# Operand sums by accumulating transfers in a hybrid attention and gMLP block on one Trainium2 core

## The chip, the cores and the metric

The kernel runs on one core of a Trainium2 chip. The core has a matrix engine (PE, with its weight loads shown as PEld), a vector engine (DVE), a scalar engine (ACT), a general engine (POOL) and a queue engine (SP), each of which works through its own instructions in order and waits on semaphores for the others. Transfers are started by an instruction of an engine's queue (here SP's and POOL's above all) and carried out by 16 DMA engines. The metric is the device time of one execution in microseconds, lower is better.

## What is computed

One layer of a streaming encoder on 1024 tokens of width 1024, in float32. Cut to what matters here (`sgo` is the gMLP branch, `a` the attention branch):

```python
h = rmsnorm(x, norm_g[l])
proj = h @ w_in[l]
q, k, v, za, u, vs, zs, gm = jnp.split(proj, IN_SPLITS, axis=-1)
a = window_sink_attention(q, k, v, att_sinks[l])
a = (a * jax.nn.silu(za)) @ w_att_out[l]
sgo = chunked_spatial_gating(gelu(u), gelu(vs), sg_w[l], sg_b[l], sg_ln_g[l], sg_ln_b[l])
sgo = (sgo * jax.nn.silu(zs)) @ w_sg_out[l]
ga, gs = jnp.split(jax.nn.sigmoid(gm + b_merge[l]), N_BRANCHES, axis=-1)
y = ga * a + gs * sgo
x = x + y @ w_o[l]
return rmsnorm(x, final_g)
```

## The kernel before

**Products.** Every large product is done by one level of Strassen's method in Winograd's form: seven products of quarters in place of eight. The moving operand of a stage (the activations, feature by token) is cut into four quarters q11, q12, q21, q22 of 512 x 512, and seven *forms* are made of them: b11 = q11, t1 = q11 - q12, t2 = -(q22 + q11 - q12), b21 = q21, t3 = q22 - q12, b22 = q22, t4 = q22 + q11 - q12 - q21. To keep float32 accuracy each form is split into a rounded high part and a low part that holds the rest (`split`, line 152: ACT writes the high part, DVE subtracts it from the source to write the low part), and a product is three matmuls per 128 rows: high by high, high by low, low by high. `product` (line 338) issues the twelve matmuls of one of the seven products.

**Pairs.** `gemm_pair` (line 355) makes two output blocks of 128 features by 1024 tokens: seven `product`s in the order b11, t1, t2, b21, t3, b22, t4, with the evictions between them (ACT: the copies to x11, x22 and x12; DVE: the sums at lines 376, 381 and 385), a call of `finish` for each of the four output tiles, and a call of `hook` after each product (seven in a pair). `split_next` (line 212), called four times in a pair, splits the weights of the pair to come into `wh` and `wl` (three buffers each). The x tiles come from a ring of five; each is free again when its store has landed. After the t2 product the x12 copy has to read the accumulator before the t3 product adds to it.

**Stages.** The work around the change has three stages of four pairs each (m = 0, 2, 4, 6). The *za stage* multiplies the input projection `hb` and applies SiLU; `finish_silu` (line 1598) multiplies each tile by the attention output, loaded as a gate tile from `at_dr`, and stores it to `a_dr` through POOL's queue. In its gaps `parts_of_s` (line 1540) makes the gMLP branch's operand: it loads the quarters of `z_dr` into `s_q`, applies SiLU and multiplies by the rows of `s1_dr`; the rows of quarter (1, 0), which is q21, come last, one by one in `multiply_row`. A table, read by (m, hook number), says when each step is written. The *s stage* multiplies the forms of `s_q` (`sb_`) and gates with the sigmoid of `gs_dr`; meanwhile the quarters of `a_dr` are loaded into `a_q`. The *a stage* multiplies the forms of `a_q` (`ab`) and gates with `ga_dr`; `y_dr` collects both.

**The boundaries.** `forms_of` (line 1506) makes the forms of a new operand, for s between the za and s stages and for a between the s and a stages. The four sums are made in place by DVE (`combine`, line 187, two instructions of 128x1024 each, seen in the profile as bq from bq and bq): q12 := q11 - q12, then q12 := q22 + q12, q11 := q12 - q11, q21 := q12 - q21. Each is followed by the splits of its form (`fill_b`, line 182). Every form has one buffer, high and low, so a fill may only be written when the last pair of the stage before has used that form. All seven are written ahead of the first pair of the new stage.

**What sets the order.** The program is written in sequence; a planner at compile time then draws up each engine's order from readiness and priority, and the position in the program is the priority. `after(second, first)` asks that `second` come behind `first` in that order. At run time each engine keeps its order and waits where something isn't ready. `want_gate` (line 1537) loads a gate tile into one of the tags g0 to g3 in turn (g0 and g1 alone in the za stage, while g2 and g3 hold the rows of `s1_dr`), and the load waits until the last reader of that tag is done.

Of the kernel before, what the change touches and what calls it, by code (L numbers as in the profile page):

```python
# [27 lines left out]
ALU = mybir.AluOpType  # L28
# [5 lines left out]
KC = D // P  # L34
# [18 lines left out]
def hybrid_tile(  # L53
# [97 lines left out]

    def split(hi, lo, src, minus=False):
        if minus:
            nc.scalar.mul(hi, src, -1.0)
            nc.vector.scalar_tensor_tensor(
                lo, src, -1.0, hi.bitcast(F32), op0=ALU.mult, op1=ALU.subtract
            )
        else:
            hi_of.append(nc.scalar.copy(hi, src))  # L159
            return nc.vector.tensor_sub(lo, src, hi.bitcast(F32))  # L160
# [20 lines left out]

    def fill_b(b, name, src, minus=None):
        hi, lo = b[name]
        for c in range(0, 4, 2):
            split(hi[:, c : c + 2, :], lo[:, c : c + 2, :], src[:, c : c + 2, :], name == "t2" if minus is None else minus)

    def combine(op, dst, a, c):
        for i in range(0, 4, 2):
            op(dst[:, i : i + 2, :], a[:, i : i + 2, :], c[:, i : i + 2, :])  # L189

# [13 lines left out]
    def begin_job():  # L206
        n = len(begun)
        if n < written[0]:
            begun.append(n)
            units.extend(jobs[n]())  # L210

    def split_next():

        if not units:
            begin_job()
        if not units:
            return
        halves, keys = units.pop(0)
        if keys[0][1] == 2:
            make_sums(term_of_x11[0] if done[0] <= 4 else None)  # L220
        hi = mtile([P, D], F32R, "wh", 3)
        lo = mtile([P, D], F32R, "wl", 3)
        if isinstance(halves, list):
            for c, half in enumerate(halves):
                split(hi[:, half_of(c)], lo[:, half_of(c)], half)
        else:
            wide = halves.shape[1]
            first = split(hi[:, 0:wide], lo[:, 0:wide], halves)
            if keys[0] == (done[0] - 1, 6) and done[0] > LAST_OF_Q + 2:
                make_sums(first)  # L230
        for c, key in enumerate(keys):
            ready[key] = hi[:, half_of(c)], lo[:, half_of(c)]
        if len(units) == 1:
            begin_job()
# [22 lines left out]
    def make_sums(first=None):  # L257

        while sums_to_make:
            sums_to_make.pop(0)(first)  # L260
# [203 lines left out]
    def get(src, m, half, bufs, tag="g"):  # L464
        g = mtile([P, HALF], F32, tag, bufs, pool)
        copy_to(g[:], place(src, m, half))
        return g
# [1035 lines left out]
            fill_b(b, name, o_loaded[name], False)  # L1503
            yield b

    def forms_of(qs):
        q11, q12, q21, q22 = (qs[k] for k in QUARTERS)
        b = {}

        def fill(name, q):  # L1510
            b.update(new_b((name,)))
            fill_b(b, name, q)

        combine(nc.vector.tensor_sub, q12, q11, q12)
        yield
        fill("b11", q11)
        fill("t1", q12)
        combine(nc.vector.tensor_add, q12, q22, q12)
        fill("t2", q12)
        fill("b21", q21)  # L1520
        combine(nc.vector.tensor_sub, q11, q12, q11)
        fill("t3", q11)
        fill("b22", q22)
        combine(nc.vector.tensor_sub, q21, q12, q21)
        fill("t4", q21)
        yield b

    ORDER = ((0, 0), (1, 1), (0, 1), (1, 0))
    gates = []

    turn = [0]

    def gtag(among=4):
        turn[0] += 1
        return f"g{turn[0] % among}"

    def want_gate(src, m, half, among=4):
        gates.append(get(src, m, half, 1, gtag(among)))

    def parts_of_s():  # L1540

        factors, of_rows = [], {}

        def rows(src, j, half):
            return src[:].rearrange("(c p) t -> p c t", p=P)[:, 4 * j : 4 * j + 4, half_of(half)]

        def load(j, half):
            s_q[j, half] = q = bq()  # L1550
            copy_to(q[:], rows(z_dr, j, half))

        def load_factors(j, half):
            factors.append(bq(0))
            copy_to(factors[-1][:], rows(s1_dr, j, half))

        def silu(j, half):
            for c in range(0, 4, 2):
                v = s_q[j, half][:, c : c + 2, :]
                after(nc.scalar.activation(v, v, AF.Silu), pace[0])  # L1560

        def multiply(j, half, c):
            v = s_q[j, half][:, c : c + 2, :]
            after(nc.vector.tensor_mul(v, v, factors[-1][:, c : c + 2, :]), term[0])

        def load_row(c, half):
            of_rows[c, half] = get(s1_dr, 4 + c, half, 1, f"g{2 + c % 2}")

        def multiply_row(c, half):
            v = s_q[1, half][:, c, :]  # L1570
            after(nc.vector.tensor_mul(v, v, of_rows[c, half][:]), term[0])

        return {
            (0, 1): [(load, 0, 0), (load_factors, 0, 0)],
            (0, 2): [(load, 1, 1)],
            (0, 3): [(load, 0, 1)],
            (0, 4): [(load_row, 0, 1), (load_row, 1, 1)],
            (0, 5): [(silu, 0, 0)],
            (0, 6): [(multiply, 0, 0, 0)],
            (0, 7): [(multiply, 0, 0, 2), (load_factors, 0, 1), (silu, 1, 1)],  # L1580
            (2, 1): [(multiply_row, 0, 1), (multiply_row, 1, 1), (load_row, 2, 1), (load_row, 3, 1)],
            (2, 3): [(silu, 0, 1)],
            (2, 6): [(multiply, 0, 1, 0), (multiply_row, 2, 1)],
            (2, 7): [(multiply, 0, 1, 2), (multiply_row, 3, 1), (load, 1, 0), (load_row, 0, 0), (load_row, 1, 0)],
            (4, 6): [(silu, 1, 0)],
            (4, 7): [(multiply_row, 0, 0), (multiply_row, 1, 0), (load_row, 2, 0), (load_row, 3, 0)],
            (6, 6): [(multiply_row, 2, 0), (multiply_row, 3, 0)],
        }


# [6 lines left out]

    def finish_silu(q, m, half):

        after(nc.vector.tensor_mul(q[:], q[:], gates.pop(0)[:]), term[0])  # L1600
        put(a_dr, m, half, q[:], nc.gpsimd)
        if of_att:
            want_gate(at_dr, *of_att.pop(0), 2)

    def part_of_s(m):
        of_za[0] += 1
# [5 lines left out]
    for m in range(0, KC, 2):  # L1612
        if m == 0:
            for _ in range(2):
                want_gate(at_dr, *of_att.pop(0), 2)
        if m == 6:
            s_forms = forms_of(s_q)
            next(s_forms)

        def finish(i, half, q, src, sign):  # L1620
            pace[0] = nc.scalar.activation(q[:], src, AF.Silu, scale=sign)
            silus.append((q, m + i, half))

        gemm_pair(hb, finish, lambda: part_of_s(m), "tp")
# [4 lines left out]

    def gate_of(src, m, i, half, col):  # L1630

        g = gates.pop(0)
        c = col + m + i
        gate = nc.scalar.activation(g[:], g[:], AF.Sigmoid, bias=bm_sb[:, c : c + 1])

        after(gate, pace[0])
        return g
# [8 lines left out]
    for m in range(0, KC, 2):  # L1646
        if m == 2:
            a_q = {}
            ahead_of_time += loads_of_quarters(a_q, a_dr)
        if m == 6:  # L1650
            a_forms = forms_of(a_q)
            next(a_forms)

        def finish(i, half, q, src, sign):
            gated(q, src, sign, gate_of(gs_dr, m, i, half, KC))
            put(y_dr, m + i, half, q[:], nc.gpsimd)
            want_gate(*((gs_dr, m + 2 + i, half) if m < 6 else (ga_dr, i, half)))

        gemm_pair(sb_, finish, part_of_loads, "tp")
    ab = next(a_forms)  # L1660


# [62 lines left out]
    for m in range(0, KC, 2):  # L1725
        if m == 6:
            written[0] += 1
            had = [mtile([P, D], F32, "s", 2) for _ in range(2)]
            for i in range(2):
                copy_to(had[i][:], y_dr[(m + i) * P : (m + i + 1) * P, :])  # L1730

        def finish(i, half, q, src, sign):
            gated(q, src, sign, gate_of(ga_dr, m, i, half, 0))
            if m < 6:
                add_to(place(y_dr, m + i, half), q[:])
                want_gate(ga_dr, m + 2 + i, half)
            else:
                nc.vector.tensor_add(q[:], q[:], had[i][:, half_of(half)])
                if half == 1:
                    last_rows[i] = q  # L1740
                copy_to(place(y_dr, m + i, half), q[:])

        if m == 2:
            ahead_of_time += [lambda name=name: load_o(name, paced) for name in list(O_SOURCES)[:4]]
        gemm_pair(ab, finish, lambda: part_of_loads(3), "tp")
    written[0] = len(jobs)

    fill = o_forms()
# [211 lines left out]
```

## Time and profile before

| | us |
|---|---|
| median of 3 runs | 908.18 |
| the runs | 908.16, 908.18, 910.48 |
| the profiled execution, its own time | 911.38 |
| the profiled execution, first to last instruction | 909.6 |

A row of the order of time gives the start, the duration, the engine, the line of the kernel, the operation, output from inputs, the shape, and in brackets how long the engine had been idle and what ended that. L346 is the matmul of `product`, L159 and L160 are the high and low parts in `split` (L155 the low part of a negated form), L189 the sums of `combine`, L204 loads through SP's queue, L462 stores, L201 and L559 accumulating transfers. A row of the waits gives the waiting engine and what it waited for, then total, count and longest. A transfer's "to landing" is counted from its issue. The granted clock in the profile is the share of PE's full speed.

### The profile page before, as it was taken

Reading aid. Unit: us, or ns where it says so; the run is one execution under the profiler, and the core shown is the slowest. Engines: PE = TensorE matmul, PEld = TensorE weight load, DVE = VectorE, ACT = ScalarE, POOL = GpSimd, SP = SyncE. Lnnn points to the kernel's source line nnn. Section 1 sums busy time; section 2 is a strip of 40 time slices with the busy share of each in tenths; the row PEclk is TensorE's granted clock in tenths of the full one; section 3 lists DMA queues with packets and bytes.
Section 4 is the critical chain, followed back from the end, with each engine's and each line's share of the span. In section 5 each row is a group of like instructions: output and inputs, shape, how many; then the busy total and the mean of one; then the engine's idle time right before and its main releaser. Section 6 shows DMA issues by size and latency. Waiting matters only on the chain.

```text
span 909.6 us, 13196 instructions
## 1 busy us (share of the span) xinstructions
PE 895.0 (98%) x4290; PEld 745.0 (82%) x4290; DVE 698.1 (77%) x1264; ACT 530.0 (58%) x1061; POOL 143.3 (16%) x205
## 2 busy tenths in 40 slices
PE   9999999999999999999999999999998999999996
PEld 6888888888888888888888888888877887888885
DVE  6869966666686778888778788647797589479996
ACT  7875533334545566767668667554674385367443
POOL 2322222203030001111111011201001111110012
PEclk9999999999999999999999999999999999999999
DMA  9997888958778667788686789899869665998632
GB/s 327 212 259 209 264 207 172 173 156 270 251 250 286 206 181 203 215 185 210 158 243 214 239 223 251 217 345 344 291 194 363 224 188 167 313 298 267 208 117 115
DMA packets 131598, 209.57 MB, mean 230 GB/s; under 512 B 12649, under 2 KB 61033, under 8 KB 131530
## 3 DMA queue, kind: packets, MB, share of 16 engines
q1 hardware_dynamic: 110072, 149.74, 50.1%
q0 software_dynamic: 21312, 58.73, 28.2%
q8 instruction: 34, 0.56, 0.3%
q14 instruction: 34, 0.28, 0.1%
q10 hardware_dynamic: 146, 0.27, 0.1%
HBM read 147.74 MB, written 86.11 MB: 257 GB/s over the span
## 4 chain that ended last, share of the span: by engine, by line
PE 87%; DVE 8%; DMA 2%; issue 2%; ACT 1%; SPq 0%; DVEq 0%; ACTq 0%
PE ps_mm L346 36%; PE ps_o L346 27%; PE ps_sc L1290 3%; PE ps_tp L346 3%; PE ps_mm L703 2%; PE ps_o L703 2%; PE ps_tp L703 2%; PE ps_o L1375 2%; PE ps_tp L1334 2%; PE ps_sc L346 2%; PE ps_tp L965 2%; DVE wl L160 1%; PE ps_sc L703 1%; DVE bq L189 1%; DMA wr<-in_w_dram 1%
## 5 line engine op out<-in xcount | busy, mean ns | idle before, releaser
L159 ACT CAST wh<-s 128x1024 fp32r<-128x1024 f32 (+1 forms) x79 | 79.3, 1006 | 95.6 <-PE ps_mm L346 51.3
L160 DVE TENSOR_TENSOR wl<-wr,wh 128x512 fp32r<-128x512 f32 (+1 forms) x77 | 72.0, 936 | 53.6 <-ACT wh L159 53.0
L160 DVE TENSOR_TENSOR wl<-s,wh 128x1024 fp32r<-128x1024 f32 (+1 forms) x79 | 92.6, 1172 | 12.2 <-ACT wh L159 11.9
L159 ACT CAST wh<-wr 128x512 fp32r<-128x512 f32 (+1 forms) x77 | 63.1, 821 | 59.3 <-PE ps_mm L346 30.7
L346 PE MATMUL ps_o<-T_t1h,wh 128*128 128x512 f32 x148 | 58.9, 398 | 0.8 <-ACT wh L159 0.7
L346 PE MATMUL ps_o<-T_b22h,wh 128*128 128x512 f32 x148 | 58.3, 394 | 0.0
L346 PE MATMUL ps_mm<-T_b11h,wl 128*128 128x512 f32 x140 | 55.4, 396 | 2.9 <-DVE wl L160 2.9
L346 PE MATMUL ps_o<-T_t1h,wl 128*128 128x512 f32 x148 | 57.9, 391 | 0.3 <-DVE wl L160 0.3
L346 PE MATMUL ps_o<-T_b22l,wh 128*128 128x512 f32 x148 | 57.9, 391 | 0.0
L346 PE MATMUL ps_o<-T_b22h,wl 128*128 128x512 f32 x148 | 57.8, 390 | 0.0
L346 PE MATMUL ps_o<-T_t1l,wh 128*128 128x512 f32 x148 | 57.7, 390 | 0.0
L1303 ACT ACTIVATE pr<-ps_sc,sm 128x192 f32<-128x192 f32 (+2 forms) x128 | 50.7, 409 | 9.0 <-DVE sm L1299 6.6
L346 PE MATMUL ps_mm<-T_b11h,wh 128*128 128x512 f32 x140 | 55.4, 395 | 0.0
L346 PE MATMUL ps_mm<-T_t4h,wh 128*128 128x512 f32 x140 | 55.2, 395 | 0.0
L346 PE MATMUL ps_mm<-T_t3l,wh 128*128 128x512 f32 x140 | 54.6, 390 | 0.6 <-DVE T_t3l L160 0.6
L346 PE MATMUL ps_mm<-T_b11l,wh 128*128 128x512 f32 x140 | 55.2, 394 | 0.0
L346 PE MATMUL ps_mm<-T_t3h,wh 128*128 128x512 f32 x140 | 55.0, 393 | 0.0
L346 PE MATMUL ps_mm<-T_t4h,wl 128*128 128x512 f32 x140 | 54.8, 391 | 0.0
L346 PE MATMUL ps_mm<-T_t3h,wl 128*128 128x512 f32 x140 | 54.7, 390 | 0.0
L346 PE MATMUL ps_mm<-T_t2h,wl 128*128 128x512 f32 x140 | 54.6, 390 | 0.0
L346 PE MATMUL ps_mm<-T_t2h,wh 128*128 128x512 f32 x140 | 54.6, 390 | 0.0
L346 PE MATMUL ps_mm<-T_t2l,wh 128*128 128x512 f32 x140 | 54.6, 390 | 0.0
(394 smaller groups left out, 2402.8 us busy)
## 6 DMA issues: line engine op xcount, KB each, us to landing
wr<-in_w_dram SPq DMA_DIRECT2D x86, 256.0 KB
sums<-in_w_dram POOLq DMA_DIRECT2D x20, 512.0 KB, 6.8
s<-sums SPq DMA_DIRECT2D x20, 512.0 KB
q_hl<-qhl SPq DMA_DIRECT2D x16, 512.0 KB
q<-q_hl SPq DMA_DIRECT2D x64, 128.0 KB
y_dr<-x POOLq DMA_DIRECT2D x28, 256.0 KB, 6.7
g<-in_w_dram POOLq DMA_DIRECT2D x12, 512.0 KB, 6.4
wr<-in_w_dram SPq DMA_DIRECT2D x11, 512.0 KB
```

The lines of the kernel that those rows point to most:

```text
L159: hi_of.append(nc.scalar.copy(hi, src))
L160: return nc.vector.tensor_sub(lo, src, hi.bitcast(F32))
L189: op(dst[:, i : i + 2, :], a[:, i : i + 2, :], c[:, i : i + 2, :])
L346: nc.tensor.matmul(acc, lt, rt, start=fresh and k == 0 and n == 0, stop=k == 3 and n == 2, skip_group_check=True,)
L703: mm = nc.tensor.matmul(acc[:], lt, rt, start=fresh and k == 0 and n == 0, stop=k == 3 and n == terms[-1], skip_group_check=True,)
L965: nc.tensor.matmul(pm[:, t * P : (t + 1) * P], xh[:, half * 4 + t, g * P : (g + 1) * P], bias[-1][1][:, g % 4, :], start=True, stop=True,)
L1290: nc.tensor.matmul(sc[:, i, k0:], q_of[:, c, i * P : (i + 1) * P], kt[:, f, k0:], start=f == 0, stop=f == 1,)
L1303: nc.scalar.activation(held_in[c, i], sc[:, i, lo:hi], AF.Exp, bias=nmax[:, c, i : i + 1], scale=-1.0, accum_out=sums[:, c, i : i + 1],)
L1334: nc.tensor.transpose(dst, pr[:, i, block * P : block * P + width], ident[:])
L1375: nc.tensor.matmul(po[:, cs], lt, rt, start=n == 0, stop=n == len(terms) - 1)
```

## The change

Two of the four sums move from DVE to accumulating transfers on POOL's queue: q12 += q22, and minus21 += q12. For the second the quarter q21 is kept negated: the last multiplication of its rows carries a factor of -1 (`times`), in `multiply_row` for s and in `finish_silu` for a, and b21's form negates it back. T2's high parts are put behind the last but one weight cast (`of_units`), the t3 sum behind t2's low parts. The t4 form is no longer made ahead of the new stage but at the third hook of its first pair (`last_form`), its high parts behind the x12 copy. The last two rows of q21 for s, with their place in the table moved from hook 6 to hook 2 of the last pair, are put behind t1's low parts; when they are done their tags g2 and g3 go to the last two `at_dr` gates (`more_gates`), and gate tags are kept in a list of free ones.

```diff
     def split(hi, lo, src, minus=False):
         if minus:
-            nc.scalar.mul(hi, src, -1.0)
-            nc.vector.scalar_tensor_tensor(
+            hi_of.append(nc.scalar.mul(hi, src, -1.0))
+            return nc.vector.scalar_tensor_tensor(
                 lo, src, -1.0, hi.bitcast(F32), op0=ALU.mult, op1=ALU.subtract
             )
...
+        of_units.append(hi_of[-1])
...
-    def forms_of(qs):
-        q11, q12, q21, q22 = (qs[k] for k in QUARTERS)
+    def forms_of(qs, behind_t1=()):
+        q11, q12, minus21, q22 = (qs[k] for k in QUARTERS)
         b = {}
 
-        def fill(name, q):
+        def fill(name, q, minus=None):
             b.update(new_b((name,)))
-            fill_b(b, name, q)
+            return fill_b(b, name, q, minus)
+
+        def add_aside(dst, src):
+            for i in range(0, 4, 2):
+                add_to(dst[:, i : i + 2, :], src[:, i : i + 2, :])
 
         combine(nc.vector.tensor_sub, q12, q11, q12)
         yield
         fill("b11", q11)
-        fill("t1", q12)
-        combine(nc.vector.tensor_add, q12, q22, q12)
-        fill("t2", q12)
-        fill("b21", q21)
-        combine(nc.vector.tensor_sub, q11, q12, q11)
+        low = fill("t1", q12)[-1]
+        for move in behind_t1:
+            after(move, low)
+        add_aside(q12, q22)
+        fill("b21", minus21, True)
+        low = fill("t2", q12)[-1]
+        for hi in hi_of[-2:]:
+            after(hi, of_units[-2])
+        add_aside(minus21, q12)
+        for sub in combine(nc.vector.tensor_sub, q11, q12, q11):
+            after(sub, low)
         fill("t3", q11)
         fill("b22", q22)
-        combine(nc.vector.tensor_sub, q21, q12, q21)
-        fill("t4", q21)
         yield b
+        fill("t4", minus21)
+        for hi in hi_of[-2:]:
+            after(hi, pace[0])
+        yield
+
+    def last_form(forms, hook):
+        calls = [0]
+
+        def hooked():
+            calls[0] += 1
+            if calls[0] == 3:
+                next(forms)
+            hook()
+
+        return hooked
+
+    def times(v, by, minus):
+        if minus:
+            return nc.vector.scalar_tensor_tensor(v, v, -1.0, by, op0=ALU.mult, op1=ALU.mult)
+        return nc.vector.tensor_mul(v, v, by)
...
-    def want_gate(src, m, half, among=4):
-        gates.append(get(src, m, half, 1, gtag(among)))
+    free_tags = ["g0", "g1"]
...
+    def want_gate(src, m, half):
+        tag = free_tags.pop(0)
+        gates.append((tag, get(src, m, half, 1, tag)))
+
+    def next_gate():
+        tag, g = gates.pop(0)
+        free_tags.append(tag)
+        return g
+
+    late_rows = []
...
         def multiply_row(c, half):
             v = s_q[1, half][:, c, :]
-            after(nc.vector.tensor_mul(v, v, of_rows[c, half][:]), term[0])
+            move = times(v, of_rows[c, half][:], half == 0)
+            after(move, term[0])
+            if half == 0 and c > 1:
+                late_rows.append(move)
+
+        def more_gates():
+            free_tags.extend(("g2", "g3"))
+            for _ in range(2):
+                want_gate(at_dr, *of_att.pop(0))
...
-            (6, 6): [(multiply_row, 2, 0), (multiply_row, 3, 0)],
+            (6, 2): [(multiply_row, 2, 0), (multiply_row, 3, 0), (more_gates,)],
...
-        after(nc.vector.tensor_mul(q[:], q[:], gates.pop(0)[:]), term[0])
+        after(times(q[:], next_gate()[:], m >= KC // 2 and half == 0), term[0])
...
-            s_forms = forms_of(s_q)
+            s_forms = forms_of(s_q, late_rows)
...
-        gemm_pair(sb_, finish, part_of_loads, "tp")
+        gemm_pair(sb_, finish, part_of_loads if m else last_form(s_forms, part_of_loads), "tp")
...
-        gemm_pair(ab, finish, lambda: part_of_loads(3), "tp")
+        hook = lambda: part_of_loads(3)
+        gemm_pair(ab, finish, hook if m else last_form(a_forms, hook), "tp")
```

More of the change, by code (lines that the diff above doesn't have):

```diff
@@ L183, in fill_b @@
         hi, lo = b[name]
-        for c in range(0, 4, 2):
-            split(hi[:, c : c + 2, :], lo[:, c : c + 2, :], src[:, c : c + 2, :], name == "t2" if minus is None else minus)
+        minus = name == "t2" if minus is None else minus
+        return [
+            split(hi[:, c : c + 2, :], lo[:, c : c + 2, :], src[:, c : c + 2, :], minus) for c in range(0, 4, 2)
+        ]
     def combine(op, dst, a, c):
-        for i in range(0, 4, 2):
-            op(dst[:, i : i + 2, :], a[:, i : i + 2, :], c[:, i : i + 2, :])
+        return [op(dst[:, i : i + 2, :], a[:, i : i + 2, :], c[:, i : i + 2, :]) for i in range(0, 4, 2)]
     jobs = []
@@ L210, in begin_job @@
             units.extend(jobs[n]())
+    of_units = []
     def split_next():
@@ L1516, in forms_of, with gtag @@
         fill("b11", q11)
-        fill("t1", q12)
-        combine(nc.vector.tensor_add, q12, q22, q12)
-        fill("t2", q12)
-        fill("b21", q21)
-        combine(nc.vector.tensor_sub, q11, q12, q11)
+        low = fill("t1", q12)[-1]
[9 more added lines that the diff above has]
+            after(sub, low)
         fill("t3", q11)
         fill("b22", q22)
-        combine(nc.vector.tensor_sub, q21, q12, q21)
-        fill("t4", q21)
         yield b
+        fill("t4", minus21)
[14 more added lines that the diff above has]
+        return nc.vector.tensor_mul(v, v, by)
     ORDER = ((0, 0), (1, 1), (0, 1), (1, 0))
     gates = []
[L1531 to L1535, printed above, removed]
-    def want_gate(src, m, half, among=4):
-        gates.append(get(src, m, half, 1, gtag(among)))
+    free_tags = ["g0", "g1"]
+    def gtag():
+        tag = free_tags.pop(0)
+        free_tags.append(tag)
+        return tag
+    def want_gate(src, m, half):
+        tag = free_tags.pop(0)
+        gates.append((tag, get(src, m, half, 1, tag)))
+    def next_gate():
+        tag, g = gates.pop(0)
+        free_tags.append(tag)
+        return g
+    late_rows = []
     def parts_of_s():
@@ L1598, in finish_silu @@
     def finish_silu(q, m, half):
-        after(nc.vector.tensor_mul(q[:], q[:], gates.pop(0)[:]), term[0])
+        after(times(q[:], next_gate()[:], m >= KC // 2 and half == 0), term[0])
         put(a_dr, m, half, q[:], nc.gpsimd)
         if of_att:
-            want_gate(at_dr, *of_att.pop(0), 2)
+            want_gate(at_dr, *of_att.pop(0))
     def part_of_s(m):
@@ L1614, in hybrid_tile @@
             for _ in range(2):
-                want_gate(at_dr, *of_att.pop(0), 2)
+                want_gate(at_dr, *of_att.pop(0))
         if m == 6:
-            s_forms = forms_of(s_q)
+            s_forms = forms_of(s_q, late_rows)
             next(s_forms)
@@ L1630, in gate_of @@
     def gate_of(src, m, i, half, col):
-        g = gates.pop(0)
+        g = next_gate()
         c = col + m + i
```

## The prediction, made before the changed kernel ran

> **What bounds the kernel now.** I read the page's busy times first, then a table of the stretches around the two changes of operand, then the first matmuls of the pairs, the waits, and the order of work on DVE and ACT.
>
> ```profile
> span 909.6 us, 13196 instructions
> PE 895.0 (98%) x4290; PEld 745.0 (82%) x4290; DVE 698.1 (77%) x1264; ACT 530.0 (58%) x1061; POOL 143.3 (16%) x205
> ...
> 665.40:684.40 19.00, 18.06 (x77) 13.90 (x75) 17.77 (x20) 13.94 (x19) 1.62 (x3) 1.00 0.73 238
> 684.40:709.30 24.90, 22.76 (x93) 18.41 (x94) 18.29 (x22) 8.86 (x14) 3.78 (x7) 0.93 0.95 345
> 709.30:728.30 19.00, 19.00 (x86) 15.73 (x85) 9.00 (x11) 7.77 (x12) 2.16 (x4) 1.00 0.63 209
> 747.30:766.40 19.10, 18.15 (x79) 14.38 (x77) 19.10 (x19) 12.08 (x16) 1.08 (x2) 1.00 0.47 156
> 766.40:787.20 20.80, 20.59 (x91) 17.04 (x92) 15.46 (x22) 7.83 (x12) 6.05 (x7) 1.00 0.99 283
> ```
>
> The columns of the table are the stretch, its length, then busy us of PE, PEld, DVE, ACT and POOL with their instruction counts, the granted clock, the DMA share and GB/s. In mid-stage (709 to 728) PE has no gap and DVE is half idle; in the first pair on a new operand (665 to 684, 747 to 766) DVE is full and PE is short. So PE bounds the kernel, and only these two boundaries let it wait. How much they cost is read off the first matmul of every second pair:
>
> ```profile
> 665.37 0.39 PE L346 MATMUL ps_mm<-T_b11h,wh 128*128 128x512 f32 x1
> 709.25 0.39 PE L346 MATMUL ps_mm<-T_b11h,wh 128*128 128x512 f32 x1
> 747.33 0.39 PE L346 MATMUL ps_mm<-T_b11h,wh 128*128 128x512 f32 x1
> 787.17 0.39 PE L346 MATMUL ps_mm<-T_b11h,wh 128*128 128x512 f32 x1
> ```
>
> From 709.25 to 747.33 two undisturbed pairs take 38.08 us: 19.04 each, 2.72 for each of the seven products. The two pairs after the first boundary (s operand) take 43.88, so it loses **5.80**; those after the second (a operand) take 39.84 and lose **1.76**. Together 7.56 us: no edit of the operands can give more. Their waits:
>
> ```profile
> 684.80 0.50 PE L346 MATMUL ps_o<-T_t1h,wh 128*128 128x512 f32 x1 [0.71 <-ACT wh L159]
> 687.28 0.79 PE L346 MATMUL ps_mm<-T_b11h,wl 128*128 128x512 f32 x1 [1.74 <-DVE wl L160]
> 687.87 0.63 PE L346 MATMUL ps_mm<-T_b11h,wh 128*128 128x512 f32 x1
> 688.29 0.63 PE L346 MATMUL ps_mm<-T_b11l,wh 128*128 128x512 f32 x1
> ...
> 678.13 0.50 PE L346 MATMUL ps_mm<-T_t3l,wh 128*128 128x512 f32 x1 [0.63 <-DVE T_t3l L160]
> 766.61 0.50 PE L346 MATMUL ps_mm<-T_b11h,wl 128*128 128x512 f32 x1 [1.11 <-DVE wl L160]
> ```
>
> Every wait is for DVE, or for an ACT cast queued behind forms that DVE feeds. After the longest gap matmuls start 0.42 apart instead of 0.23, with the clock of that stretch at 0.93: six of them are some 1.2 of the 5.80, and go with the gap.
>
> **The DVE chain, and what is removed.**
>
> ```profile
> 653.53 2.36 DVE L160 TENSOR_TENSOR T_t1l<-bq,T_t1h 128x1024 fp32r<-128x1024 f32 x2 [0.36 <-ACT T_t1h L159]
> 656.41 1.22 DVE L189 TENSOR_TENSOR bq<-bq,bq 128x1024 f32<-128x1024 f32 x1
> 661.62 2.35 DVE L155 SCALAR_TENSOR_TENSOR T_t2l<-bq,T_t2h 128x1024 fp32r<-128x1024 f32 x2
> 671.71 0.69 DVE L1600 TENSOR_TENSOR x<-x,g 128x512 f32<-128x512 f32 x1 [1.14 <-DMA g<-at_dr]
> 673.45 2.35 DVE L189 TENSOR_TENSOR bq<-bq,bq 128x1024 f32<-128x1024 f32 x2
> 675.72 1.22 DVE L160 TENSOR_TENSOR T_b22l<-bq,T_b22h 128x1024 fp32r<-128x1024 f32 x1
> 680.27 2.35 DVE L189 TENSOR_TENSOR bq<-bq,bq 128x1024 f32<-128x1024 f32 x2
> 682.54 0.68 DVE L160 TENSOR_TENSOR wl<-wr,wh 128x512 fp32r<-128x512 f32 x1
> 683.14 2.35 DVE L160 TENSOR_TENSOR T_t4l<-bq,T_t4h 128x1024 fp32r<-128x1024 f32 x2
> 686.01 1.22 DVE L160 TENSOR_TENSOR wl<-wr,wh 128x1024 fp32r<-128x1024 f32 x1
> ```
>
> Two sums on DVE take 2.27 (673.45 to 675.72). Four of the six remaining ones at a boundary go: the t2 sum (656.41 and its twin) and the t4 sum (680.27): 4.54 us, at each boundary. The gate waited for at 671.71 (1.14) is now loaded earlier, through the two tags that the late rows set free, so that wait goes too at the first boundary: 5.7 in all. The last item, the weights' low part at 686.01, is done at 687.2 and wanted at 665.37 + 19.04 + 0.23 = 684.6; 5.7 earlier is 681.5, 3.1 us to spare. T_t3l (first half done about 678.1, wanted 676.5) gains the t2 sum and the gate, 3.4: in time by 1.8. T_t4l's first half, done near 684.4, goes to 678.7 against 681.9. At the second boundary the low part waited for at 766.61 comes 4.54 earlier. So the first-order gain is all of 7.56.
>
> **What is added: the transfers.** Four accumulating transfers of 512 KB at each boundary, on POOL's queue, SBUF to SBUF. The same shape runs early in this kernel:
>
> ```profile
> L559 POOL DMA_DIRECT2D T_t3h<-T_t4h x2: 854/856/858, 24.1 to 27.9; - x2
> ...
> T_t3h<-T_t4h POOLq DMA_DIRECT2D x2, 512.0 KB, 7.2
> T_t3l<-T_t3h POOLq DMA_DIRECT2D x2, 512.0 KB, 4.7
> ...
> L201 POOL DMA_DIRECT2D y_dr<-x x12: 850/859/1213, 767.5 to 807.4; - x12
> DMA to landing us min/median/max: 6.7/7.8/9.6
> ...
> L300 POOL DMA_DIRECT2D sums<-in_w_dram x40: 515/807/2082, 66.5 to 176.5; - x40
> DMA to landing us min/median/max: 4.4/7.3/14.3
> ```
>
> An issue is 0.86, a landing L between 4.7 and 14.3; I take 7.2, the same shape and the slower of its two rows. A leg (two issues, then the landing) is 1.7 + L = 8.9. First leg: T_t1l ends at 655.9 and frees q12, which is summed at 664.8. T_t2h, put behind the weight cast at 662.67 (done 663.7), takes 2.0 and T_t2l ends near 668; t2's product starts at 665.37 + 2 x 2.72 = 670.81. Before, T_t2l ended at 663.9, so it becomes later and still has 2.8 to spare. While t2 is out, DVE has other work, at 0.60 for 128x512 (682.54 to 683.14) and 1.13 for 128x1024: two late rows (1.2), the low parts of three weight tiles (0.6 + 2 x 1.13), b21's two (2.27), and four sums and gatings of the pair (2.4): 8.7 us against 9.9 until T_t2h's first half is there. About 1.2 us of DVE idle is new, out of the 3.1 to spare.
>
> Second leg: it needs the first (664.8) and b21's forms, so minus21 holds t4 at 673.7, about when T_t4h may start: it now waits for the x12 copy, after t2's product ends at 673.5. Then 2.0 of casts and a last low part: t4 ready near 677.5, wanted 681.69. At the second boundary T_t1l ends at 737.9 (735.50 + 2.36), the product of t4 starts at 763.65: the same 26 us for the same chain.
>
> ```profile
> 735.50 2.36 DVE L160 TENSOR_TENSOR T_t1l<-bq,T_t1h 128x1024 fp32r<-128x1024 f32 x2 [0.36 <-ACT T_t1h L159]
> 662.67 1.05 ACT L159 CAST wh<-s 128x1024 fp32r<-128x1024 f32 x1 [0.54 <-ACT x L1621]
> L462 POOL DMA_DIRECT2D a_dr<-x x16: 540/540/555, 604.6 to 672.7; - x16
> a_dr<-x POOLq DMA_DIRECT2D x16, 256.0 KB, 5.8
> ```
>
> The bounds of L: at 4.7 nothing changes in the sum. At 9.1 the DVE's spare time is gone; the t4 chain, 2(1.7 + L) + 2.1, fills the 26 us at L = 10.25. Beyond, each us costs 2 at each boundary.
>
> What stands behind the waiting instructions: on POOL, the a_dr and y_dr stores wait while the second leg waits for the first. A store that goes out at 666.5 lands 5.8 later at 672.3; its x tile is wanted by the x12 copy at 673.5, which must start by 675.6 before t3's product adds into the same bank. If the store also queues behind a megabyte of sums (L more) it lands near 679 and PE loses up to 3.4. On ACT, the sigmoid gates and casts for the next pair wait behind T_t2h and T_t4h. I put 0.25 on each boundary for these. The negations cost nothing: the negated low part (L155, 2.35 for two) lasts as long as the plain one (2.36), and they replace instructions one for one. The late rows only move, from 666 to 656.
>
> [...]
>
> **The sum.** The profiled execution took 911.38, 1.78 around its span; 7.56 less twice 0.25 gives 904.3. The median before is 908.18, 3.2 under it, and the same 7.06 gives **901.1**.
>
> **Rivals.**
> 1. *Part of the gain goes into new waits.* L near 10, or an order in which DVE stands for T_t2l with other work behind it: DVE late by 10 - 9.1 = 0.9, and the x tile ring's 3.4 once: 908.18 - 7.56 + 4.3 = 904.9. For it: landings of 7.8 to 9.6 on L201, DMA share 0.73 and 0.95 in these stretches. Against: the same shape's 7.2 and 4.7 were taken at a busy start too.
> 2. *Slower: the two legs in series come too late for t4.* Place: T_t4h at the head of ACT's queue, next pair's casts behind it. From L = 10.25 + 7.56/4 = 12.1 it costs more than all that is gained. At 13.2, between that and L300's longest: 4 x 2.95 = 11.8 lost, 908.18 - 7.56 + 11.8 = 912.4. Against: only L300's longest is that long, and those read HBM.
> 3. *It doesn't act*: the freed DVE time is taken by other work due at the same moment, PE waits on ACT instead: 908.2. Against: in the waits ACT comes last once, 0.71, and that cast stands behind T_t4h, which DVE feeds.
>
> **Chances.** A measurement of this kernel tells about 0.3% (2.7 us) from no change. Forecast 0.56, rival 1 0.21, rival 2 0.17, rival 3 0.06. Rival 1 is faster by 3.3, just over the bound: I count 0.17 of its 0.21 as faster, so faster 0.73, same 0.10, slower 0.17. The floor is 908.18 - 7.56 = 900.6 and some spread of the runs: 899.8. Upward the range takes in rivals 1 and 3 and the mild end of 2: 909.3. The forecast's own range is 900.2 to 903.
>
> **What would show it.** The first-matmul distances fall from 43.88 and 39.84 to about 38.3 each; the clock after the first boundary stays at 1.00; the group of DVE sums (bq from bq, bq) has 8 instead of 16; POOL shows 8 new transfers landing in 5 to 9 us; T_t2l ends near 668 and T_t4l before 679 at the first boundary. A PE wait on T_t2 or T_t4, or a first-matmul distance over 42, would make the forecast wrong; landings over 12 us would make it rival 2.

## The result, and the profile after

| | before | after |
|---|---|---|
| median of 22 runs each | 909.04 us | 906.58 us |
| range | 907.53 to 911.63 | 903.73 to 909.31 |
| profiled execution, its own time | 911.38 | 908.01 |
| its span | 909.6 | 906.2 |

The ratio is 0.9967, with a 95% interval of 0.9959 to 0.9976: faster, by 2.5 us in the medians where the forecast said 7.1. One execution of the changed kernel, in e12 below, took 1279.19 us at a granted clock of 0.656; it stands in none of the figures here, so e12 has no losses to show. The page of the kernel after, its busy times:

```profile
span 906.2 us, 13224 instructions
PE 893.7 (99%) x4290; PEld 746.1 (82%) x4290; DVE 690.1 (76%) x1256; ACT 530.0 (58%) x1061; POOL 149.9 (17%) x213
```

DVE lost eight instructions and 8.0 us of work, POOL gained eight transfers. The first matmuls of the pairs that stood in the prediction, now:

```profile
664.97 0.39 PE L350 MATMUL ps_mm<-T_b11h,wh 128*128 128x512 f32 x1
...
707.23 0.39 PE L350 MATMUL ps_mm<-T_b11h,wh 128*128 128x512 f32 x1
...
745.31 0.39 PE L350 MATMUL ps_mm<-T_b11h,wh 128*128 128x512 f32 x1
...
784.25 0.39 PE L350 MATMUL ps_mm<-T_b11h,wh 128*128 128x512 f32 x1
```

Two undisturbed pairs, 707.23 to 745.31, take 38.08 as before. The two after the first boundary take 42.26, a loss of 4.18 (before 5.80), those after the second 38.94, a loss of 0.86 (before 1.76). Together 5.04 instead of 7.56: the 2.52 between them is about what the medians show (2.46). So the question is what the 5.04 are made of. PE's waits around both boundaries, and what two ACT copies wait for there (engine, output and line, what it waited for; total, count, longest):

```profile
PE ps_mm L350 <- ACT x L375: 2.8, 2, 2.3
ACT x L375 <- DMA a_dr<-x: 2.7, 1, 2.7
ACT x L372 <- DMA a_dr<-x: 2.2, 1, 2.2
ACT x L375 <- DMA y_dr<-x: 2.2, 1, 2.2
```

No wait for DVE is left. L375 is the x12 copy, L372 the x22 copy (the lines moved by four). Both wait for an x tile whose store, to `a_dr` or `y_dr`, has not landed. In order of time, ACT, then PE, then POOL at the first boundary:

```profile
669.13 0.59 ACT L368 COPY x<-ps_mm 128x512 f32<-128x512 f32 x1
671.93 0.60 ACT L372 ACTIVATE x<-ps_o 128x512 f32<-128x512 f32 x1 [2.21 <-DMA a_dr<-x]
672.43 1.99 ACT L159 CAST T_t3h<-bq 128x1024 fp32r<-128x1024 f32 x2
674.32 0.62 ACT L159 CAST wh<-wr 128x512 fp32r<-128x512 f32 x1
677.64 0.59 ACT L375 COPY x<-ps_mm 128x512 f32<-128x512 f32 x1 [2.71 <-DMA a_dr<-x]
678.12 1.99 ACT L159 CAST T_t4h<-bq 128x1024 fp32r<-128x1024 f32 x2
```

```profile
675.63 0.39 PE L350 MATMUL ps_tp<-T_b21h,wl 128*128 128x512 f32 x1
678.28 0.50 PE L350 MATMUL ps_mm<-T_t3h,wh 128*128 128x512 f32 x1 [2.26 <-ACT x L375]
678.61 0.59 PE L350 MATMUL ps_mm<-T_t3l,wh 128*128 128x512 f32 x1
679.01 0.63 PE L350 MATMUL ps_mm<-T_t3h,wl 128*128 128x512 f32 x1
```

```profile
654.67 0.88 POOL L202 DMA_DIRECT2D bq<-bq  x1 [5.13 <-DMA g<-s_dr]
655.80 0.87 POOL L202 DMA_DIRECT2D bq<-bq  x1 [0.25 <-DMA g<-at_dr]
660.99 0.85 POOL L202 DMA_DIRECT2D bq<-bq  x1 [4.32 <-DVE x L385]
661.74 0.68 POOL L466 DMA_DIRECT2D a_dr<-x  x1
665.35 0.85 POOL L202 DMA_DIRECT2D bq<-bq  x1 [2.94 <-DVE wl L160]
665.90 1.42 POOL L466 DMA_DIRECT2D a_dr<-x  x2
667.56 0.55 POOL L466 DMA_DIRECT2D a_dr<-x  x1 [0.23 <-DVE x L1557]
```

PE should have begun t3's product at 675.85. The copy that reads the accumulator first had to start by 675.3, and started at 677.64, because its x tile came back only then. PE stood for 2.3 us, and nine of the matmuls after that follow 0.33 to 0.43 apart instead of 0.23: 2.4 us of lateness became 4.2. The stores stand behind the second leg's transfers on POOL. These wait for the first leg: each goes out 0.52 us after the landing of the first leg's same half (at 660.47 and 664.83), though the rows name a DVE instruction that ended at about that time. So the second store, whose tile DVE had finished at 663.8, went out at 665.90, and then took 11.7 us to land. The landing of the stores, from the answers for `a_dr` in the same stretch, first before, then after:

```profile
DMA to landing us min/median/max: 3.9/5.6/6.6
```

```profile
DMA to landing us min/median/max: 10.1/11.7/11.8
```

And the DMA engines, second number from the right in the stretches of before, then of after:

```profile
654.00:660.00 6.00, 6.00 (x28) 4.95 (x27) 6.00 (x7) 4.38 (x7) 0.00 (x0) 1.00 0.75 264
660.00:666.00 6.00, 6.00 (x28) 4.99 (x27) 6.00 (x8) 5.46 (x7) 0.54 (x1) 1.00 0.41 131
666.00:672.00 6.00, 6.00 (x28) 4.95 (x28) 4.77 (x7) 3.67 (x6) 1.08 (x2) 1.00 0.78 237
```

```profile
654.00:660.00 6.00, 6.00 (x29) 4.95 (x28) 6.00 (x8) 4.38 (x7) 1.75 (x2) 1.00 1.02 270
660.00:666.00 6.00, 6.00 (x28) 4.99 (x27) 6.00 (x9) 4.58 (x7) 2.07 (x4) 1.00 1.04 275
666.00:672.00 6.00, 6.00 (x28) 4.95 (x27) 5.89 (x7) 3.79 (x6) 1.87 (x4) 1.00 1.07 308
```

Shares of 0.41 to 0.78 have become more than 1. The share adds up packet times; at 1 or more I call the engines full.

### The profile page after: what moved, and what is told of

Its sections match the earlier page's. It is cut to its first block, busy times and chain, and to the rows that moved or that the text cites. A ratio compares the mean times of both kernels' runs of the same rounds, so it can differ in the third digit from the quotient of the medians.

```text
span 906.2 us, 13224 instructions
## 1 busy us (share of the span) xinstructions
PE 893.7 (99%) x4290; PEld 746.1 (82%) x4290; DVE 690.1 (76%) x1256; ACT 530.0 (58%) x1061; POOL 149.9 (17%) x213
## 3 DMA queue, kind: packets, MB, share of 16 engines
q1 hardware_dynamic: 110072, 149.74, 49.9%
## 4 chain that ended last, share of the span: by engine, by line
PE 87%; issue 5%; DMA 5%; POOL 1%; DVE 1%; ACT 1%; POOLq 0%; DVEq 0%; ACTq 0%
PE ps_mm L350 36%; PE ps_o L350 27%; PE ps_sc L1294 3%; PE ps_mm L707 3%; PE ps_o L707 2%; PE ps_tp L707 2%; PE ps_o L1379 2%; PE ps_sc L350 2%; PE ps_tp L1338 2%; PE ps_tp L350 2%; DMA bq<-bq 2%; PE ps_tp L969 2%; DMA a_dr<-x 1%; PE ps_sc L707 1%; DMA y_dr<-x 1%
```

## The experiments

Theory A: the x tiles come back late, since their stores travel behind the second leg in POOL's queue. Theory B: the sums or forms themselves are late. Theory C: the DMA engines are full, whatever the order. Theory D: the two legs in series are the tight chain. In the table "loss" is the distance from the first matmul of the new stage's first pair to that of its third, less 38.08; the last column is the profiled span less both losses.

| kernel | ratio to before, 95% | loss at the first, the second boundary | span less losses |
|---|---|---|---|
| before | 1 | 5.80, 1.76 | 902.0 |
| the change | 0.9967 (0.9959 to 0.9976) | 4.18, 0.86 | 901.2 |
| e1 | 0.9933 (0.9918 to 0.9947) | 2.53, 0.00 | 900.9 |
| e2 | 0.9932 (0.9915 to 0.9948) | 1.05, 0.00 | 901.6 |
| e3 | 1.0026 (1.0016 to 1.0036) | 5.83, 1.76 | 901.0 |
| e4 | 0.9993 (0.9984 to 1.0003) | 4.56, 1.74 | 901.4 |
| e5 | 1.0042 (1.0027 to 1.0058) | 6.72, 4.94 | 901.2 |
| e6 | 0.9978 (0.9962 to 0.9995) | 2.92, 0.00 | 901.5 |
| e7 | 0.9940 (0.9926 to 0.9954) | 1.34, 0.69 | 902.5 |
| e8 | 0.9998 (0.9987 to 1.0008) | 7.58, 0.02 | 900.1 |
| e9 | 0.9949 (0.9936 to 0.9961) | 0.75, 0.00 | 901.3 |
| e10 | 1.0091 (1.0077 to 1.0105) | 8.59, 8.61 | 901.3 |
| e11 (the change) | 0.9953 (0.9940 to 0.9965) | 1.30, 0.87 | 901.1 |
| e12 (the change) | 0.9959 (0.9945 to 0.9972) | - | - |
| e13 (as e1) | 0.9955 (0.9941 to 0.9970) | 2.43, 0.01 | 902.0 |
| e14 (as e2) | 0.9938 (0.9925 to 0.9952) | 1.09, 0.00 | 901.6 |
| e15 (as e7) | 0.9948 (0.9934 to 0.9961) | 0.88, 0.69 | 901.9 |

Without the losses every span is 900.1 to 902.5, where the losses run from 0.75 to 17.2: in the profiles the two boundaries hold what the kernels differ by, but for some 2 us. e1 to e4, e5 to e8, e9 to e11 and e12 to e15 ran side by side.

**e1, the x tiles freed by DVE.**

```diff
-        after(times(q[:], next_gate()[:], m >= KC // 2 and half == 0), term[0])
-        put(a_dr, m, half, q[:], nc.gpsimd)
+        g = next_gate()
+        to = g if m >= 6 else q
+        after(times(q[:], g[:], m >= KC // 2 and half == 0, to[:]), term[0])
+        put(a_dr, m, half, to[:], nc.gpsimd)
```

(and the same in the s stage's `finish` for m == 6)

> Edit: in the last pair of the za stage and of the s stage the gated tile is written into its gate's tile and stored from there, so that an x tile is free once DVE has read it, not when the store has landed. Theory A (the x12 copy waits for an x tile whose store travels behind the sums on POOL's queue): the waits of ACT on stores at the x22 and x12 copies go, PE waits under 0.5 us in both first pairs, distances of first matmuls 38.1 to 38.8 at both boundaries, ratio to before 0.991 to 0.993. Theory B (the sums or forms themselves are late, the x tile only came last): PE waits for T_t2, T_t3, T_t4 or wl instead, first distance over 41, ratio 0.996 or more.

The waits for stores are gone, at the second boundary the loss too. At the first, 2.53 stay, in another place. PE's and the gates' waits there, of e1:

```profile
PE ps_mm L350 <- DVE wl L160: 2.2, 1, 2.2
ACT g L1686 <- DMA g<-gs_dr: 2.0, 1, 2.0
```

A gate tile is now held until the store lands, the gate's next load goes out later, and ACT waits for it with the casts of weights behind it. So the x tiles were the change's loss, and holding another buffer in their place moved the lateness into the second pair. The forecast of distances 38.1 to 38.8 held at the second boundary alone. But e1 changed a second thing. The first gate loads of the s stage, in the change and then in e1, and the stores of e1:

```profile
661.46 2.66 SPq L205 DMA_DIRECT2D g<-gs_dr  x2
669.67 0.33 SPq L205 DMA_DIRECT2D g<-gs_dr  x1
a_dr<-g POOLq DMA_DIRECT2D x4, 256.0 KB, 7.9
```

In e1 the stores stand behind the second leg just as in the change, and yet they land after 7.9 us in the median (the change 11.7): with the gate loads 8 us later there is less beside them (264 GB/s from 666 to 672, in the change 308). Their place in the queue alone does not make 10 to 12.

**e2, the stores out of POOL's order.**

```diff
-        put(a_dr, m, half, q[:], nc.gpsimd)
+        put(a_dr, m, half, q[:], nc.sync if m >= 6 else nc.gpsimd)
...
-            put(y_dr, m + i, half, q[:], nc.gpsimd)
+            put(y_dr, m + i, half, q[:], nc.sync if m == 6 else nc.gpsimd)
```

> Edit: the stores of the last pair of the za stage (a_dr) and of the s stage (y_dr) go through SP's queue instead of POOL's. Theory A (they are late because they follow the sums in one queue): they land 4 to 6 us after their issue, the x12 copy no longer waits or waits under 0.5 us, ratio 0.991 to 0.994. Theory C (the 16 DMA engines are full, in whatever queue the stores go): they land after 8 to 11 us as now, and the x12 copy still waits about 2 us, ratio about 0.9967 as the change.

The ratio and the x12 copy are A's: it starts at 675.36 right behind ACT's casts, on time, and the losses fall to 1.05 and 0. But the x22 copy still waits 2.9 for a store (ACT's waits of e2):

```profile
ACT x L372 <- DMA a_dr<-x: 2.9, 1, 2.9
```

The first two stores go out through SP:

```profile
661.70 0.89 SPq L466 DMA_DIRECT2D a_dr<-x  x1
664.03 0.32 SPq L466 DMA_DIRECT2D a_dr<-x  x1
```

The copy starts at 672.46, so whichever it waited for took 8 to 11 us; in the change it started as the first store landed (671.9), and if it waits for the first here too, that one took 10.7. That part is C's: out of POOL's order, into engines whose share is 1.02 to 1.08 in e2 as well. What e2 gained for the x12 copy is above all the issue: the second store goes out at 664.03 instead of 665.90, 1.9 us sooner, of the 2.4 by which the copy was late in the change.

**e3, the tiles of e1 in the kernel before.** The edit of e1's diff, with the plain product.

> Edit: the kernel before, with the gated tiles of those two last pairs written into the gate tiles as in e1. Theory A with DVE as the bound of before: no change, distances 43.9 and 39.8, ratio 0.999 to 1.001. If the x tiles bounded the kernel before as well: first distance 41 or less, ratio 0.997 or less.

Its losses are those of before, 5.83 and 1.76, so before was not bound by x tiles. The median is 2.4 us slower than before's, which the losses don't show; where that comes from is open.

**e4, both sums back on DVE.**

```diff
-        add_aside(q12, q22)
+        combine(nc.vector.tensor_add, q12, q22, q12)
...
-        add_aside(minus21, q12)
...
+        combine(nc.vector.tensor_add, minus21, q12, minus21)
         yield b
```

> Edit: the changed kernel with both sums back on DVE (t2's sum where its transfer stood, t4's after b22's form), and all the rest of the change kept: the negated quarter, the late rows behind t1, four gate tags, t4's form in the next pair. If the transfers carry the gain: DVE is full again in both first pairs, distances 42 to 44 and 39 to 40, ratio 0.998 to 1.000. If the gates and the order carry it: ratio 0.9967 or less, with no store that comes late (landing 5 to 6 us).

The gates and the order are worth 1.24 us of loss at the first boundary, and in the runs nothing that can be told from zero. The transfers carry the change.

**e5, the second leg behind the stores.**

```diff
-        def add_aside(dst, src):
+        def add_aside(dst, src, first=None):
             for i in range(0, 4, 2):
-                add_to(dst[:, i : i + 2, :], src[:, i : i + 2, :])
+                move = add_to(dst[:, i : i + 2, :], src[:, i : i + 2, :])
+                if first is not None:
+                    after(move, first)
...
-        add_aside(minus21, q12)
+        add_aside(minus21, q12, stored[-1])
```

(`stored` collects the stores of `put`)

> Edit: the changed kernel with the two transfers of the second sum (minus21 += q12) put behind the last of the four stores of the last pair in POOL's order. Theory A (the x tiles come back late because their stores travel behind the second leg): stores land in 6 to 9 us instead of 10 to 12, the x12 copy waits under 0.5 us, T_t4 still in time, losses at the two boundaries (distance of first matmuls less 38.08) 0 to 1.5 and 0 to 0.3, ratio 0.992 to 0.995. Theory C (the DMA engines are full whatever the order, share above 1.0 from 654 to 678): x12 still waits 1.5 us or more, ratio 0.996 or more. Theory D (the two legs in series are the tight chain): PE waits for T_t4, loss over 3.

Stores land after 5.6 to 6.7 us, with the engines as full as in the change (1.02 to 1.08): a full share does not make them late by itself, nor, by e1, does the place behind the second leg. At the first boundary they took 9 us or more where the second leg and the gate loads were both under way with them (the change 10.1 to 11.8, e11 9.1 to 10.8, e10 10.7 to 11.2, the first store of e2 as read above), and 5.6 to 7.2 where the leg came later or not at all (e5, e7), 7.9 in the median where the gate loads did (e1). That fits these runs; neither was varied by itself. The x12 copy comes at 673.63 without a wait. And then D holds, which nothing had shown so far (ACT's and PE's rows of e5):

```profile
678.49 1.05 ACT L159 CAST T_t4h<-bq 128x1024 fp32r<-128x1024 f32 x1 [4.28 <-DMA bq<-bq]
681.52 1.04 ACT L159 CAST T_t4h<-bq 128x1024 fp32r<-128x1024 f32 x1 [1.98 <-DMA bq<-bq]
```

```profile
PE ps_mm L350 <- ACT wh L159: 4.2, 1, 4.2
```

The second leg goes out at 668.4 instead of 661 and 665, its last half is there at 681.5 when t4 is due, and the weights' casts for the next pair stand behind it on ACT. The kernel is slower than before.

**e6, e1 and e2 together.**

> Edit: e1 and e2 together, results in the gate tiles and stored through SP's queue. e1 lost 2.5 at the first boundary to a weights' low part that stood behind sigmoid gates loaded late, e2 1.05 to the x22 copy. If the x tiles are all that is left of the change's loss, both go: losses 0 to 0.5 and 0, ratio 0.9915 to 0.993. If the late gate loads come from the full DMA engines and not from POOL's order, the loss in the second s pair stays at 1 to 3, ratio 0.993 to 0.995.

The loss in the second s pair stays, 2.92: PE waits 2.6 for a weights' low part and ACT 3.0 for gate loads. Taking the stores off POOL did not bring the gates earlier. Its median, 907.96, lies some 3 us above what its losses say (909.53 - 7.56 + 2.92 = 904.9); as for e3 this is open.

**e7 and e8, one sum by transfers.** Of e4's two edits, e7 makes the second alone and e8 the first alone.

> Edit: only the first sum (q12 += q22) by transfers, the second (minus21 += q12) on DVE behind b22's form. DVE gets back 2.27 of 4.54 and the DMA engines carry half the sums. If the gain of a sum is the DVE time that it frees and its price the late stores: stores land in 6 to 9 us, losses 2.0 to 3.5 and 0 to 1, ratio 0.994 to 0.997. If already one leg makes the stores late: x12 waits 2 us or more, ratio 0.998 or more.

> Edit: only the second sum (minus21 += q12) by transfers, the first (q12 += q22) on DVE in its old place. Same arithmetic of DVE as e7: losses 2.0 to 3.5 and 0 to 1, ratio 0.994 to 0.997 if the second leg alone leaves the stores time; if it is the second leg that makes them late (theory A): x12 or x22 waits 1.5 us or more and the ratio is above e7's.

e7: stores land after 5.7 to 7.2 us, no copy waits for one at the first boundary, and DVE is late again by only 0.7 (PE for wl), so that the losses, 1.34 and 0.69, are smaller than expected at the first. The first leg alone does not make the stores late, and with half of the transfers the kernel is no slower than the change. e8: with the t2 sum on DVE the low parts of b21 behind it come later, and the second leg, which needs them, goes out at 666.3 and 669.2; T_t4h waits 3.3 for its last half and PE 3.5 for a cast behind it. The stores, three of the four ahead of that leg at the first boundary (3.6 to 6.4 us to land; 9.9 for the fourth, behind its first half), did not hold the copies; my expectation for e8 named the wrong wait.

**e9, one tile of e2 into its gate.** e2, and `to = g if (m, half) == (6, 0) else q` for the za stage's last pair.

> Edit: e2 (the stores of both last pairs through SP's queue), and of the za stage's last pair the first tile alone is written into its gate's tile, so that one x tile more is free for the x22 copy. If the 2.9 us wait of the x22 copy for a store is what e2 still loses at the first boundary: that wait goes, loss there 0 to 0.6 (e2: 1.05) and 0 at the second, ratio 0.991 to 0.993. If something else holds e2 there: loss 1 or more, ratio as e2's 0.9932.

The wait at x22 is gone and a gate load of the second pair is late instead: 0.75 of loss, just above the 0 to 0.6 expected. The ratio, 0.9949, is not told from e11's beside it.

**e10, t4's form ahead of the pair.**

```diff
+        fill("t4", minus21)
         yield b
-        fill("t4", minus21)
-        for hi in hi_of[-2:]:
-            after(hi, pace[0])
         yield
```

> Edit: the changed kernel with t4's form made ahead of the new stage's first pair, as before, instead of at its third hook. On ACT its casts then stand ahead of the x11 copy and wait there for the second leg. If the second leg lands near 673 as its issue at 661 to 665 and a landing of 8 to 10 say: the x11 copy comes 4 to 5 us late, PE waits for it before t2's product, losses 5 to 9 and 2 to 5, ratio 0.999 to 1.005. If the place of t4's form doesn't matter: losses 4.2 and 0.9 as in the change, ratio 0.9967.

PE's wait in e10 at the first boundary:

```profile
PE ps_mm L350 <- ACT x L368: 5.5, 1, 5.5
```

T_t4h stands ahead of the x11 copy and waits there until 675.6 for the second leg. The loss is 8.6 at each boundary, 17 us in all, more than the 2 to 5 expected at the second. So the last form's place inside the pair is no ornament: without it the kernel is 0.9% slower than before.

**e11 to e15, side by side.**

> Edit: none, the changed kernel beside the other two on the same chip. Theory A: losses 4 to 4.5 and 0.7 to 1, ratio 0.996 to 0.9975, and e9 below it by 3 to 4 us. If the difference between the variants came from the chip and not from the edit: ratio within 0.001 of e9's.

> Edit: none, the changed kernel beside the three below on one chip. Theory A says that its x12 copy misses its time by an amount that differs from execution to execution (2.4 us in one profile, 0.35 in another): loss 2 to 5 at both boundaries together, ratio 0.9945 to 0.9975, and a wider spread of its runs than of the next three.

> Edit: as e1. If the x tiles cost the change 2 us or more in its median run, this one is 1.5 us or more below e12: ratio 0.992 to 0.9945. If the late stores cost only in single executions: within 1 us of e12.

> Edit: as e2. As e13: 1.5 us or more below e12, ratio 0.992 to 0.9945, if the order of the stores behind the second leg costs in the median run; within 1 us of e12 if not.

> Edit: as e7, the first sum alone by transfers. If the second leg gives back in late stores what it frees on DVE: no slower than e12, ratio 0.993 to 0.9965. If the second leg is worth its 2.27 us of DVE: above e12 by 1 us or more.

In e11's profile the change's stores land after 9.1 to 10.8, its x12 copy starts at 675.66, 0.35 late, and the first loss is 1.30 instead of 4.18: a store that lands 1 to 2 us sooner is worth 2.9. That would account for some of the 5.6 us over which its 22 runs range (before: 4.1). The expectation for e11 missed: this profile took just the median of its five runs, 905.13, so that there the change's usual loss was nearer 2.2 than 5, and e9 is only 0.6 below it. In e12 the change's runs range over 3.7 us, those of the next three over 1.8 to 2.7, as expected. On one chip e14 is 1.8 us below e12 by the medians (903.45 against 905.2), though the two intervals still overlap; e13 is level with e12. Its expectation gave that for late stores that cost only in single executions; e13's own loss of 2.4 explains it as well, and the runs don't decide between the two. e15 is level with e12 too, within the intervals, so the second leg gives back about what it frees. The best version that was measured twice is e2, the change with those eight stores through SP: 0.9932 and 0.9938 on two chips.

## Why the prediction was right or wrong

- *DVE bounds the boundaries; four of its instructions go at each.* Right: sums of `combine` fell from 16 to 8, and no PE wait for DVE is left. e3 shows that the x tiles did not bound before.
- *The room is 7.56.* Right as a bound: e1 and e2 lose nothing at the second boundary, and the span less losses is the same for all kernels within 2.4 us. No version lost less than 0.75 at the first.
- *The gate's wait of 1.14 goes.* Right in size: e4, which has that edit and the new order without the transfers, loses 1.24 less at the first boundary; the two were not tried apart.
- *L = 7.2 for a sum.* The eight landed after a median of 8.7. T_t2h started at 663.23 right behind the weight cast, earlier than forecast, so the first leg was in time for it. T_t4 was in time too: in the change T_t4h waits for no transfer.
- *"A store that goes out at 666.5 lands 5.8 later" and "I put 0.25 on each boundary for these."* This is the step that failed, by its size: the late x tiles, put at 0.25 for each boundary, cost 4.18 at the first and 0.86 at the second in the profile. The place, the tile and the deadline (675.6, measured 675.3) were right, and the store that held the x12 copy went out at 665.90, near the 666.5 assumed. But the price of "up to 3.4" if the store queues behind the sums was the measured case: the stores took 10.1 to 11.8. I took for the sum the landing of a store in an emptier queue, when the POOL rows that I had laid out put the second leg ahead of it. With 3.4 at the first boundary the sum would have been 908.18 - 7.56 + 3.65 = 904.3, where the measured ratio gives 905.2 on the same 908.18.
- *What was left out* is the load on the DMA engines. I read shares of 0.73 and 0.95 and added no transfer time to them; with the two legs the share is above 1 from 654 to 678, and by e1 and e5 a store's landing there hangs on what runs beside it (medians of 7.9 and 6.4, in the change 11.7). And lateness was priced one for one, though the rows of before showed slower matmuls after a gap (0.42 apart instead of 0.23): 2.4 us late cost 4.2. The sign that was named, a first distance over 42, came (42.26).
- *Rival 1* (part of the gain goes into the x tile ring, 904.9) is what happened, in its x tile half. That 905.2 was measured is partly luck: the 0.9 for DVE did not occur, and the slow matmuls, which were not in it, did. *Rival 2* (t4 too late, slower than before) did not, but e5 and e10 bring it about by moving one thing, and e8 gives back by it all that it gains. The second leg's last half landed at 675.2, 1.5 us later than the forecast 673.7.
- *An issue is 0.86.* Right: the eight took 0.845 to 0.889 us, the first four of them beside a DVE that was busy 23.1 of the 24 us from 654 to 678.

## What to carry to other kernels

Work that moved from an engine to transfers was paid for twice here: in the DMA engines' time (from 654 to 672 a share of 0.41 to 0.78 became 1.02 to 1.07), which must be added to a share that is already there, and in the position of everything issued behind it in the same queue, which waits with it for what it waits for (the second store went out at 665.90, in e2, through SP, at 664.03). Before costing such a move, list the buffers whose return hangs on a store behind it, each with its deadline, and take the landing of a store that runs beside such transfers, in whatever queue, not that of one in an emptier machine (here 10.1 to 11.8 us against the 3.9 to 6.6 of before). Where a wait ends within a microsecond of its deadline, give it the price of the stall and of the slow matmuls after it, not its mean (here 4.2 us for 2.4 of lateness).

## What the runs showed of the hardware

The accumulating transfers occupied the DMA engines about twice as long for a byte as the other queue's transfers, 166 GB/s against 331, as an estimate from the queues' totals. The queues' rows (packets, MB, share of 16 engines), before and after:

```profile
q1 hardware_dynamic: 110072, 149.74, 50.1%
q0 software_dynamic: 21312, 58.73, 28.2%
```

```profile
q1 hardware_dynamic: 110072, 149.74, 49.9%
q0 software_dynamic: 22464, 62.93, 31.1%
```

The eight sums added 4.20 MB and 0.311 x 906.2 - 0.282 x 909.6 = 25.3 us of all 16 engines, 166 GB/s, or 3.2 us each, if the rest of that queue took as long as before; the 149.74 MB of the other queue went at 331 GB/s. From issue to landing the sums, beside other traffic, took 5.8 to 10.0 us at the first boundary.

Two waits of PE of about the same length were followed by different paces. After 2.26 us in the change nine matmuls ran at the slow pace (granted clock 0.66 from 678 to 683; in detail 0.50 from 678.63 to 682.05 and 1.00 on either side); after 2.18 us in e1 the next ones ran nearly at full pace, 0.23 to 0.24 apart from the second on, and the mean granted clock from 640 to 812 was 1.00 (in the change 0.99):

```profile
678.00:683.00 5.00, 4.72 (x14) 3.74 (x15) 2.96 (x3) 4.97 (x7) 0.00 (x0) 0.66 0.79 276
```

```profile
697.65 0.50 PE L350 MATMUL ps_mm<-T_t3h,wl 128*128 128x512 f32 x1 [2.18 <-DVE wl L160]
697.99 0.40 PE L350 MATMUL ps_mm<-T_t3h,wh 128*128 128x512 f32 x1
698.23 0.40 PE L350 MATMUL ps_mm<-T_t3l,wh 128*128 128x512 f32 x1
```

The slow stretch of the change lasted 3.4 us. What sets the two waits apart is not shown: no run here moved such a wait.
